# Two 32-byte pads that move the normalized inputs and the feed-forward tiles by 32 and 64 bytes

## The chip, the cores and the metric

One NeuronCore of a Trainium2 chip runs the kernel. The metric is the time of one execution on the device in microseconds (us): 2235.31 us is the median of three runs before the change (2234.43 to 2235.77).

## The reference

A sequence of 256 positions and a context of 256 positions, each of width 1024 in float32, go through two transformer layers and then a second block of two hybrid layers. A layer of the first block is feed-forward, attention, feed-forward, and every feed-forward (four in all) is

```
def _ffn_sublayer(h, mod, g_pre, g_post, w_in, w_out):
    shift, scale, gate = mod
    u = _modulate(_rmsnorm(h, g_pre), shift, scale)
    a, b = jnp.split(u @ w_in, 2, axis=-1)
    y = (jax.nn.silu(a) * b) @ w_out
    return h + MACARON_W * gate * _rmsnorm(y, g_post)
```

with an inner width of 2816. The first layer's attention is a differential one, the second's a neighbourhood one; shift, scale and gate come from a conditioning vector through large matrices (the "ada" work). The last feed-forward is computed for the sequence alone, the other three for sequence and context. The hybrid layers project a normalized input to several small mixers (latent attention, a gated delta rule, block attention), join their outputs and add the result. The output is the normalized sequence, 256 by 1024.

## The kernel before, in words

**The products.** Every large product is made in the float32r type from numbers that are split in two: a high part (a rounded copy, made by ScalarE) and a low part (what is left, made by VectorE; both in `split`, lines 155 and 156). `mm3` (line 190) then issues three matmuls: high by high and high by low on the same stationary tile, and then low by high on the low tile. All of them are recorded in `mm` (line 161), so the profile puts them at L164, L168 or L179, whatever their stage; the tiles' names tell them apart. The stationary operand of 128 by 128 is loaded anew for each matmul, so PE's matmuls (PE) and its weight loads (PEld) have the same count. The moving operand is 512, 258 or 256 columns wide, one float32r word a column, and lies in one unbroken run of a partition.

**Who is stationary and who moves.** In the feed-forward's first product (`part`, line 466), in the attention projections and in the hybrid layers' projections the weight tile `w` is stationary and the normalized input `u` moves. In the feed-forward's second product (`into`, line 500) `w` is stationary and the feed-forward's tile `b` moves. In the attention's output projection (`out_proj`, line 635) `w` is stationary and `o` moves. In `v_tiles` (line 602) it is the other way round: `u` is stationary and `w` moves.

**Stages.** A feed-forward for both halves first makes some inner tiles for the sequence alone (256 columns), then, when the context's input is normalized, for the context alone (256), then both at once (`wide`, 512); after 12 of 22 inner tiles it makes the first part of the second product (512), after the rest the remaining parts for each half (256). The last feed-forward and the hybrid layers move 256 columns, the last feed-forward's first product 258 (two more columns carry the shift). Weights come by SP's DMA queue into four raw tiles of 512 KB each and are split into eight `w` tiles.

**Where tiles lie.** SBUF space is given to pools in the order in which they are opened (lines 89 to 95), and each pool's tiles follow one another; a tile of any size takes a multiple of 32 bytes. So the small constants of the pool `cst` end at a multiple of 32, and all that follows starts there. By the program as it is built, a tile's start in its partition, modulo 128 bytes, is before the change:

| tiles | start modulo 128 |
|---|---|
| `w` (split weights) and `raw` | 64 |
| `u` (normalized inputs, pool `up`), `y` and `v` (pool `yp`), `c4`, `s`, `r256`, `r512` (pool `tmp`) | 64 |
| `b` of the feed-forward (opened by `space`, line 110) | 96 |
| `o`, `kl`, `qk`, `pT` of both attentions (opened by `space` too) | 96 |
| `ra`, `cb` (ada work, pool `cbp`) | 96 |
| `gd`, `sel`, `lvl` of the hybrid layers | 64 |
| `ident` | 32 |

All these tiles but the smallest have sizes that are multiples of 128 bytes, and the columns at which matmuls enter them too, so a matmul's moving operand starts at the tile's own remainder. PSUM's tiles are in a memory of their own.

**The order of work.** The order of instructions on each engine is that of the program; a tile's reuse waits for its last reader. The tiles named here are made once for each use, by `tile` of their pool.

Of the kernel before, what the change touches and what calls it, by code (L numbers as in the profile page):

```python
# [23 lines left out]
F = mybir.dt.float32  # L24
# [19 lines left out]
class Split:  # L44


    def __init__(self, hi, lo):
        self.hi, self.lo = hi, lo
# [35 lines left out]
class Net:  # L84
    def __init__(self, es, tc, I, O, stages=None, dump=None):
        self.tc, self.nc, self.I, self.O = tc, tc.nc, I, O
        self.stages, self.dump = stages, dump
        self.anchor = self.last_load = None
        self.cst = self.pool(es, "cst", 1)
        self.wp = self.pool(es, "wp", N_W)  # L90
        self.rawp = self.pool(es, "rawp", N_RAW)
        self.up = self.pool(es, "up", 8)
        self.yp = self.pool(es, "yp", 4)
        self.tmp = self.pool(es, "tmp", 3)
        self.col = self.pool(es, "col", 4)
        self.nps = self.pool(es, "nps", 1, space=bass.MemoryType.PSUM)
# [12 lines left out]
    @contextmanager  # L109
    def space(self, name, n):  # L110

        with ExitStack() as es:
            self.bp = self.pool(es, name, n)
            yield

# [1439 lines left out]
```

## Time and profile before

| | |
|---|---|
| median of the runs | 2235.31 us |
| the profiled execution, its own time | 2234.45 us |
| its span, first to last instruction | 2232.3 us |
| mean granted clock of TensorE, as a share of full speed | 0.993 |
| PE busy | 2169.9 us, 97% |
| VectorE (DVE) busy | 1589.2 us, 71% |
| ScalarE (ACT) busy | 1118.0 us, 50% |

A row of a group of instructions gives line, engine and operation, the tiles it writes and reads, shapes and count, then the busy time, the mean of one in ns, and the idle time ahead of them. A piece of the chain that ended last gives start, length (both us), engine, tile and line, and after "x" the number of instructions in it. Where the chain stays on PE, the length divided by the number is the pace, the time from one matmul's start to the next; the "mean ns of one" is longer, since a matmul is counted until its last result is out, while the next is already running.

### The profile page before, as it was taken

The page shows a single profiled execution, that of the slowest core. Times are in us where ns is not written, and L with a number is a line of the kernel's source. Part 1 is how long each engine was busy: PE and PEld are TensorE (multiplying, and loading weights), DVE is VectorE, ACT ScalarE, POOL GpSimd, SP SyncE. Part 2 cuts the span into 40 slices and gives each one's busy share as a digit, 9 for nine tenths or more (in the row PEclk, how much of TensorE's full clock was granted, in tenths as well). Part 3 has the DMA queues.
Part 4 walks back from the last instruction along what each step waited for, and adds up shares of the span by engine and source line. Part 5 has one row for each costly group of instructions (what it writes and reads, how often), then busy time and mean ns, then how long its engine had stood idle before and what let it go on. Part 6 is the DMA issues. An engine that isn't in the chain of part 4 may idle for free.

```text
span 2232.3 us, 33427 instructions
## 1 busy us (share of the span) xinstructions
PE 2169.9 (97%) x13010; PEld 1876.6 (84%) x13010; DVE 1589.2 (71%) x2899; ACT 1118.0 (50%) x1841; POOL 6.5 (0%) x33
## 2 busy tenths in 40 slices
PE   7999999999999999999999999999999989999998
PEld 3888889877789888889988889977789989888986
DVE  7877674869978876767844454956665668977985
ACT  4422223668867322236622223668754448457644
POOL 0000000000000000000000000000000000000000
PEclk9999999999999999999999999999999999999999
DMA  8555553431134655544554453432335543324321
GB/s 300 198 181 192 182 183 130 156 104 48 38 104 164 228 202 189 193 165 149 185 177 153 168 170 133 152 132 88 109 129 190 175 164 123 114 81 138 120 99 57
DMA packets 96166, 332.77 MB, mean 149 GB/s; under 512 B 12772, under 2 KB 15462, under 8 KB 96008
## 3 DMA queue, kind: packets, MB, share of 16 engines
q1 hardware_dynamic: 96008, 330.64, 43.5%
q8 instruction: 102, 1.67, 0.3%
q14 instruction: 56, 0.46, 0.1%
HBM read 329.55 MB, written 1.05 MB: 148 GB/s over the span
## 4 chain that ended last, share of the span: by engine, by line
PE 79%; ACT 9%; DVE 9%; issue 1%; DMA 1%; SPq 0%; DVEq 0%; ACTq 0%
PE ab L164 36%; PE ac L164 16%; PE ac L168 7%; PE pj L164 5%; PE ab L179 5%; PE gd L164 3%; PE n L164 2%; PE ab L168 2%; ACT w L155 2%; DVE w L156 1%; PE at L164 1%; DVE y L375 1%; ACT c L772 1%; PE gd L168 1%; PE pj L168 1%
## 5 line engine op out<-in xcount | busy, mean ns | idle before, releaser
L155 ACT ACTIVATE w<-raw 128x1024 fp32r<-128x1024 f32 x466 | 489.7, 1053 | 789.5 <-PE ab L164 269.8
L164 PE MATMUL ab<-u,w 128*128 128x512 f32 (+2 forms) x4320 | 870.9, 361 | 4.1 <-ACT u L438 4.1
L164 PEld LDWEIGHTS ab<-u,w 128*128 128x128 f32 x4320 | 728.8, 189 | 126.0 <-ACT u L438 4.5
L156 DVE TENSOR_TENSOR w<-raw,w 128x1024 fp32r<-128x1024 f32 x466 | 567.6, 1220 | 319.6 <-ACT w L155 312.7
L164 PE MATMUL ac<-b,w 128*128 128x512 f32 (+1 forms) x1152 | 235.9, 366 | 0.0
L164 PEld LDWEIGHTS ac<-b,w 128*128 128x128 f32 x1152 | 195.6, 188 | 39.6
L168 PE MATMUL ac<-b,w 128*128 128x256 f32 x1680 | 200.3, 280 | 0.0
L168 PEld LDWEIGHTS ac<-b,w 128*128 128x128 f32 x1680 | 198.2, 188 | 0.8
L164 PE MATMUL pj<-u,w 128*128 128x256 f32 (+1 forms) x1200 | 158.8, 288 | 5.6 <-ACT u L438 4.4
L293 DVE SCALAR_TENSOR_TENSOR ra<-ra,cb 128x1024 f32<-128x1024 f32 x130 | 158.3, 1222 | 5.1 <-ACT cb L1349 2.2
L164 PEld LDWEIGHTS pj<-u,w 128*128 128x128 f32 (+1 forms) x1200 | 148.2, 190 | 10.5 <-ACT u L438 5.0
L179 PE MATMUL ab<-u,w 128*128 128x256 f32 x1152 | 147.1, 289 | 9.1 <-ACT u L155 7.8
L179 PEld LDWEIGHTS ab<-u,w 128*128 128x128 f32 x1152 | 143.6, 196 | 10.7 <-ACT u L155 8.1
L293 DVE SCALAR_TENSOR_TENSOR c<-ra,cb 128x1024 f32<-128x1024 f32 x98 | 118.8, 1220 | 12.9 <-ACT cb L1349 6.4
L484 DVE TENSOR_TENSOR s<-s,ab 128x512 f32<-128x512 f32 (+1 forms) x78 | 47.1, 604 | 90.6 <-PE ab L164 90.0
L164 PE MATMUL ac<-w,u 128*128 128x512 f32 x384 | 90.4, 394 | 0.0
L164 PEld LDWEIGHTS ac<-w,u 128*128 128x128 f32 x384 | 71.7, 188 | 15.4 <-DVE u L156 0.4
L164 PE MATMUL n<-r,ones 128*128 128x256 f32 (+1 forms) x216 | 73.2, 449 | 7.4 <-DVE r L62 3.3
L155 ACT ACTIVATE b<-s 128x512 fp32r<-128x512 f32 (+1 forms) x100 | 53.5, 535 | 28.3 <-DVE s L484 21.2
L156 DVE TENSOR_TENSOR b<-s,b 128x512 fp32r<-128x512 f32 (+1 forms) x100 | 56.3, 563 | 3.1 <-ACT b L155 2.9
L164 PEld LDWEIGHTS n<-r,ones 128*128 128x128 f32 x216 | 36.5, 196 | 20.1 <-DVE r L62 9.6
L64 ACT ACTIVATE r<-h 128x512 f32<-128x512 f32 x56 | 35.0, 627 | 31.3 <-DVE h L379 10.6
(290 smaller groups left out, 2297.1 us busy)
## 6 DMA issues: line engine op xcount, KB each, us to landing
raw<-in_fin SPq DMA_DIRECT2D x194, 512.0 KB, 3.3
raw<-in_fout SPq DMA_DIRECT2D x112, 512.0 KB, 3.3
ra<-in_ada SPq DMA_DIRECT2D x72, 512.0 KB, 4.2
ra<-in_ada0r SPq DMA_DIRECT2D x58, 512.0 KB, 3.2
raw<-in_w SPq DMA_DIRECT2D x54, 512.0 KB, 3.3
raw<-in_da_qk SPq DMA_DIRECT2D x16, 512.0 KB, 3.2
raw<-in_na_qk SPq DMA_DIRECT2D x16, 512.0 KB, 3.3
raw<-in_w2o SPq DMA_DIRECT2D x16, 512.0 KB, 3.2
```

The costliest lines, as they stand in the source:

```text
L64: net.nc.scalar.activation(s, x, AF.Square)
L155: self.nc.scalar.activation(hi, x, AF.Copy)
L156: self.anchor = self.nc.vector.tensor_tensor(lo, x, hi.bitcast(F), op=OP.subtract).ins.name
L164: return mm(out, lhsT, rhs, start=start, stop=stop)
L168: ins = mm(out, lhsT, rhs, start=start and "first" not in bank, stop=stop and bank["done"] == n)
L179: ins = mm(out, lhsT, rhs, start=start, stop=stop)
L293: ins = nc.vector.scalar_tensor_tensor(junk, w, 1.0, self.cb[:, j], op0=OP.mult, op1=OP.mult, accum_out=self.mod[l][:, m, t, j:j + 1])
L375: ins = nc.vector.scalar_tensor_tensor(yy[:, t], yy[:, t], cols[:, k:k + 1], r, op0=OP.mult, op1=OP.mult)
L484: nc.vector.tensor_tensor(s, s, pb, op=OP.mult)
L772: nc.scalar.activation(e[:, j, :nk], s, AF.Exp, bias=mx[:, j:j + 1], accum_out=sm[:, j:j + 1])
```

## The change

Two pads of 8 float32 (32 bytes in each partition) are made as pools of their own, each with one small memset on GpSimd (POOL). The first stands in front of the pool `up`; everything that is opened later moves up by 32 bytes with it. The second stands in front of the feed-forward's pool and is made anew in each of the four feed-forwards; only `b` moves by it, a further 32 bytes. `w`, `raw` and the constants keep their places.

```
+        pad = self.pool(es, "pad", 1).tile([128, 8], F, name="pad", tag="pad")
+        tc.nc.gpsimd.memset(pad, 0.0)
         self.up = self.pool(es, "up", 8)
...
         with ExitStack() as es:
+            if name == "ffn":
+                pad = self.pool(es, "ffnp", 1).tile([128, 8], F, name="pad", tag="pad")
+                self.nc.gpsimd.memset(pad, 0.0)
             self.bp = self.pool(es, name, n)
```

So `u`, `y`, `v`, `c4`, `s`, `r256`, `r512` and the hybrid layers' `gd`, `sel`, `lvl` go from 64 to 96 modulo 128, `ra`, `cb` and the attentions' `o`, `kl`, `qk`, `pT` from 96 to 0, and `b` from 96 to 32.

## Rows read from the trace of the kernel before

**Rows 1.** The page: busy time of each engine, and the granted clock in 40 slices.
```profile
PE 2169.9 (97%) x13010; PEld 1876.6 (84%) x13010; DVE 1589.2 (71%) x2899; ACT 1118.0 (50%) x1841; POOL 6.5 (0%) x33
...
PEclk9999999999999999999999999999999999999999
```

**Rows 2.** Busy us (and count) of PE, PEld, DVE, ACT, POOL by stretch; granted clock.
```profile
60.00:400.00 340.00, 340.00 (x1706) 289.07 (x1706) 239.67 (x349) 108.05 (x145) 0.00 (x0) 1.00 0.52 178
...
1830.00:2060.00 230.00, 217.98 (x1578) 194.70 (x1579) 189.51 (x443) 146.29 (x247) 1.62 (x16) 0.99 0.33 111
```

**Rows 3.** The page: the chain that ended last, share of the span by line.
```profile
PE ab L164 36%; PE ac L164 16%; PE ac L168 7%; PE pj L164 5%; PE ab L179 5%; PE gd L164 3%; PE n L164 2%; PE ab L168 2%; ACT w L155 2%; DVE w L156 1%; PE at L164 1%; DVE y L375 1%; ACT c L772 1%; PE gd L168 1%; PE pj L168 1%
```

**Rows 4.** The chain in order of time, its longest pieces: start, length, instructions.
```profile
71.21 108.83 PE ab L164 x480
180.03 67.20 PE ac L164 x288
...
356.07 29.87 PE ac L168 x256
...
419.69 16.13 PE ac L164 x71
...
1072.02 40.31 PE ab L179 x336
...
1739.91 59.51 PE ab L164 x480
```

**Rows 5.** The chain in two short stretches: output projection, and gates of a hybrid layer.
```profile
641.73 4.55 PE ac L168 x39
...
1864.87 2.70 PE at L164 x23
```

**Rows 6.** Groups by line and form: matmuls with `u`, `b`, `w` or `o` moving.
```profile
L164 PE MATMUL ab<-u,w 128*128 128x512 f32 x3096 | 716.8, 390 | 0.0
L164 PE MATMUL ac<-b,w 128*128 128x512 f32 x864 | 202.1, 395 | 0.0
L168 PE MATMUL ac<-b,w 128*128 128x256 f32 x1680 | 200.3, 280 | 0.0
L164 PE MATMUL pj<-u,w 128*128 128x256 f32 x1152 | 152.2, 288 | 5.6 <-ACT u L438 4.4 <-DVE w L156 0.7 <-DVE r L1159 0.5
L179 PE MATMUL ab<-u,w 128*128 128x256 f32 x1152 | 147.1, 289 | 9.1 <-ACT u L155 7.8 <-DVE u L156 1.0 <-DVE w L156 0.2
L164 PE MATMUL ab<-u,w 128*128 128x258 f32 x1056 | 132.9, 286 | 4.1 <-ACT u L438 4.1
L164 PE MATMUL ac<-w,u 128*128 128x512 f32 x384 | 90.4, 394 | 0.0
L168 PE MATMUL ac<-o,w 128*128 128x256 f32 x384 | 47.6, 282 | 0.0
L164 PE MATMUL ac<-b,w 128*128 128x256 f32 x288 | 33.8, 279 | 0.0
L168 PE MATMUL gd<-u,w 128*128 128x256 f32 x192 | 29.9, 292 | 4.7 <-DVE w L156 2.7 <-ACT w L155 2.1
...
L168 PE MATMUL ab<-o,w 128*128 128x256 f32 x192 | 28.7, 298 | 2.3 <-ACT w L155 2.3
...
L164 PE MATMUL ab<-u,w 128*128 128x256 f32 x168 | 22.3, 282 | 0.0
```

**Rows 7.** Groups by line and form: VectorE with `c` or `ra`, and POOL's memsets.
```profile
L293 DVE SCALAR_TENSOR_TENSOR ra<-ra,cb 128x1024 f32<-128x1024 f32 x130 | 158.3, 1222 | 5.1 <-ACT cb L1349 2.2 <-DMA ra<-in_ada 0.5
L293 DVE SCALAR_TENSOR_TENSOR c<-ra,cb 128x1024 f32<-128x1024 f32 x98 | 118.8, 1220 | 12.9 <-ACT cb L1349 6.4 <-DMA ra<-in_ada0r 3.3 <-DMA ra<-in_ada 3.2
...
L1015 POOL MEMSET xp<- 128x3 f32 x24 | 2.4, 102 | 487.3 <-DVE r L1020 234.3 <-PE ac L168 223.0 <-DVE w L996 8.1
```

**Rows 8.** PE's transposes of line 200: nanoseconds least, median and most.
```profile
L200 PE MATMUL ac<-ident,e x128: 270/272/273, 1488.5 to 1602.7; 128*128 128x128 f32 x128
...
L200 PE MATMUL at<-ident,r x48: 270/272/333, 1969.8 to 2213.2; 128*128 128x128 f32 x48
```

## The prediction, made before the changed kernel was run

> **What bounds the kernel now.** I read the page's busy times first. PE is busy 97% of the span, VectorE 71%, ScalarE 50%, and the clock is granted in full in every slice, which is the 2.4 GHz level [rows 1]. By stretch it is the same: in the first feed-forward PE is busy in all of the 340 us while VectorE has 100 us to spare; in a hybrid layer PE still has 218 of 230 us, but with gaps [rows 2]. The shares of the chain say which work has to change for the end to move: it runs through PE's products of every kind, half of it through those with `u` and `b` moving [rows 3]. So only the pace of matmuls can matter much, and the reader should look at it, not at the mean of one.
>
> **The pace depends on where the moving operand starts.** The chain's long pieces stay on PE, so length by count is the pace [rows 4, 5]:
> - `u` moving from 64, 512 columns: 108.83 / 480 = 226.7 ns;
> - `b` from 96, 512 columns: 67.20 / 288 = 233.3 ns;
> - `u` from 64, 256 columns: 40.31 / 336 = 120.0 ns;
> - `b` from 96, 256 columns: 29.87 / 256 = 116.7 ns; `o` from 96: 4.55 / 39 = 116.7 ns;
> - `w` moving from 64 with `u` stationary, 512 columns: 16.13 / 71 = 227.2 ns.
>
> At 2.4 GHz 512 columns are 213.3 ns and 256 are 106.7 ns. From 64, then, a matmul costs some 13.4 ns over its columns at either width; from 96 it costs 20 ns at 512 and 10 ns at 256, that is, a share. That `o` goes with `b` and the moving `w` goes with `u`, though loop order and PSUM tiles differ, is what makes me put it down to the start. So 96 is worse than 64 for the wide matmuls by 6.6 ns, and better for the narrow ones by 3.3 ns.
>
> **The sum.** After the change `u` starts at 96, as `b` does now, with the same `w` under it; this half has its price in the rows.
> 1. *512 columns, `u` from 64 to 96.* 3,096 matmuls [rows 6]. Of these 2,592 are in three feed-forwards (the chain has six pieces like the first one, with 480, 480, 336, 480, 336 and 480), wholly on the path: 2,592 x 6.6 ns = +17.1 us. The other 504 are attention projections, between waits for ScalarE and VectorE; +3.3 us, and I take half: +1.7.
> 2. *256 columns, `u` from 64 to 96.* 1,152 with L179, 1,152 with `pj`, two groups of 192 (`gd` and a `pj` one) and two of 168 [rows 6]: 3,024 x 3.3 ns = -10.0 us. L179 holds 5% of the span's chain, some 112 us of 147 busy, and `pj` at L164 the same of 152 [rows 3, 6], so three quarters are on the path: -7.5. Ends: -4 (the feed-forwards alone) and -10.
> 3. *258 columns, `u` from 64 to 96.* 1,056 matmuls [rows 6]; the pace is 59.51 / 480 = 124.0 ns, with a gap at each change of tile in it [rows 4]. At most they come down to 116.7 x 258 / 256 = 117.6 ns, -6.8 us; nothing is the other end. I take the narrow ones' 3.3 ns: -3.5.
> 4. *`b` from 96 to 32.* 864 matmuls of 512 columns and 1,680 + 288 = 1,968 of 256 [rows 6], nearly all on the path. No float32r operand of before starts at 32. Below: no stream is faster than a column a cycle, so -(20 x 864 + 10 x 1,968) ns = -37 us. Above: another step as from 64 to 96 for the wide and the other way for the narrow, +6.6 x 864 + 3.3 x 1,968 = +12.2 us. Which row is nearest? Starts that are multiples of 64 (`u`, `w`) share one behaviour, and 32 and 96 are both 32 over such a multiple; a start that splits each piece of 64 bytes would do so alike at both. I take the row of 96: 0.
> 5. *`o` from 96 to 0.* 384 + 192 matmuls of 256 columns [rows 6]; by the same parity 0 goes with 64: 576 x 3.3 ns = +1.9 us; the other end is 0.
> 6. *`w` moving, `u` stationary from 64 to 96.* 384 matmuls [rows 6]. The moving start stays, so 0; if the stationary start counts as much, 384 x 6.6 ns = 2.5 us either way. Against that: the transposes move `ident` from 32, and take 272 ns with stationary `e` at 96 as with `r` at 64 [rows 8]. The remaining two-pass float32 matmuls take twice the time a column; I leave them at 0.
> 7. *VectorE, ScalarE, DMA.* The ada product costs 1,222 ns with its output at 96 and 1,220 with it at 64 [rows 7]; both engines have room [rows 2]; 0.
> 8. *The pads.* Five memsets, each by the row of the smallest ones 0.1 us [rows 7], on POOL, which is busy 6.5 us in all [rows 1]. Behind one in the queue stand the memsets of `kl` and `xp`; a feed-forward's pad may wait until what lay there before is free, and so may they, but attention or hybrid layers come after a whole feed-forward's work. If that cover were gone, it would be 5 x 0.1 us. 0.
>
> Sum: 17.1 + 1.7 - 7.5 - 3.5 + 0 + 1.9 = **+9.7 us**. The profiled execution's own 2234.45 us (its span and 2.2 us around it) becomes 2244.2; it lies 0.9 us under the median of the runs, so against that I say 2235.3 + 9.7 = **2245.0 us**, 0.43% slower. Two runs of this kernel that differ by under 0.2%, 4.5 us, cannot be told from no change.
>
> **Rivals.**
> - *32 is the best start of all (faster).* Place: the second product, `ac<-b,w`. The loss per column may grow with the start within 128 bytes, so that 32 is as far below 64 as 64 is below 96: 512 columns at 226.7 - 6.6 = 220.1 ns, -13.2 x 864 = -11.4 us; the narrow ones, where the loss is then less than at 96, at perhaps 113.4, -3.3 x 1,968 = -6.5. With the rest as above: 2245.0 - 17.9 = 2227.1 us. It decides from 9.7 us / 2,832 = 3.4 ns a matmul on. For it: 64 and 96 do differ by a share of the columns. Against it: the narrow ones are better at 96 than at 64, which no growth with the start explains; and with only 8 columns to load, `u` from 64 runs at 2.70 / 23 = 117.4 ns [rows 5], so part of the narrow 120 ns is the load, not the start. Chance 0.25.
> - *The start is not the cause (no change).* Then `b` is slower at 512 columns for its loop (a new PSUM tile after every six matmuls) and nothing moves: 2235.3 us. For it: all rows of `b` are of that loop. Against it: `w` moving changes its PSUM tile after every three, and has 227 ns. The Trainium skill says as much as this rival: its page "SBUF — State Buffer", section "Who interferes with whom", has PE with two independent read ports, one for the moving operand and one for the loads, and waiting on nobody, and its specifications know only lines of 16 bytes, of which 32, 64 and 96 are all multiples; "TensorE: Matmul & The Clock Gate", section "Wait — 56ns, not 53.3ns?", gives one pace for 512 columns, 215.7 ns. The trace agrees with neither, as it has 226.7 and 233.3 ns [rows 4]. Chance 0.15.
> - *32 is worse than 96 (slower still).* The price is the upper end of step 4: 2245.0 + 12.2 = 2257.2 us. For it: nothing but that two neighbouring starts already differ. Chance 0.13.
>
> **How the numbers follow.** My forecast has 0.47. Its own range is 2238 to 2250 us, from the ends of steps 1 to 3, 5 and 6. To leave out no more than 2 in 10 the range must reach the faster rival and most of the third: 2226 to 2256 us. Faster by over 0.2% comes from the first rival and a little of the forecast's edge (0.27); within 0.2% from the second and the forecast's lower end, should the narrow gains all count (0.18); slower from the rest (0.55).
>
> **What would show it.** In the profile after: `ab<-u,w` of 512 columns in pieces of 480 at 112.0 us where it was 108.8 shows step 1; the L179 piece of 336 at 39.2 us step 2; `ac<-b,w` still at 67.2 us for 288 and 29.9 us for 256 step 4. The forecast is wrong if the `u` pieces keep 226.7 ns (then the start alone is not the cause), or if `b` at 32 falls under some 230 ns at 512 or 113 ns at 256.

## The result, and the profile after

The changed kernel takes 2256.69 us (median of 4, 2254.71 to 2257.44) where the kernel before takes 2235.54 (4 runs, 2234.43 to 2237.47). The medians are 21.2 us apart; the ratio of the runs is lower, 1.0085 with an interval of 1.0073 to 1.0097, which is 19.0 us and 16.3 to 21.7. The forecast was 9.7 us slower; the range ended at 2256, and the rival "32 is worse than 96" had 2257.2.

The page after: PE has 24.4 us more to do than before [rows 1], the other engines the same, and the clock is at nine tenths or more in every slice, as before; its mean is 0.990 of full speed, where it was 0.993.

```profile
PE 2194.3 (97%) x13010; PEld 1880.1 (83%) x13010; DVE 1589.0 (70%) x2899; ACT 1118.4 (50%) x1841; POOL 6.9 (0%) x38
...
PEclk9999999999999999999999999999999999999999
```

The chain in order of time answers to [rows 4]. The program is five lines longer, so L164, L168 and L179 of before are L169, L173 and L184 here.

```profile
70.47 111.99 PE ab L169 x480
182.47 67.21 PE ac L169 x288
...
361.68 30.71 PE ac L173 x256
...
426.13 16.55 PE ac L169 x71
...
749.90 78.39 PE ab L169 x336
...
1086.58 39.20 PE ab L184 x336
...
1762.60 59.32 PE ab L169 x480
```

Line by line against before: wide `u` from 108.83 to 111.99 us; wide `b` as it was; narrow `b` from 29.87 to 30.71; the moving `w` of `v_tiles` from 16.13 to 16.55; narrow `u` from 40.31 to 39.20; the 258 columns from 59.51 to 59.32. The starts of the same pieces say where the time came: 0.7 us early at the first, then 2.4 us late, 5.6, 6.4, 14.6 at 1086.58 and 22.7 at 1762.60; the two spans are 23.4 us apart. So nearly all of it is lost in the first block; from the piece of 258 columns to the end, which is mostly the hybrid layers, the two traces differ by 0.7 us only, to which step 2 below comes back.

Groups by form, for wide `u`, the hybrid layers' projections and the attentions' output projections (columns as in [rows 6]), and the pads on POOL:

```profile
L169 PE MATMUL ab<-u,w 128*128 128x512 f32 x3096 | 735.6, 396 | 0.0
...
L169 PE MATMUL pj<-u,w 128*128 128x256 f32 x1152 | 149.3, 285 | 5.9 <-ACT u L443 4.4 <-DVE w L161 0.9 <-DVE r L1164 0.6
...
L173 PE MATMUL ac<-o,w 128*128 128x256 f32 x384 | 47.9, 282 | 0.0
...
L173 PE MATMUL ab<-o,w 128*128 128x256 f32 x192 | 30.6, 311 | 2.3 <-ACT w L160 2.3
...
L173 PE MATMUL gd<-u,w 128*128 128x256 f32 x192 | 30.5, 296 | 4.0 <-ACT w L160 2.1 <-DVE w L161 2.0
...
L117 POOL MEMSET pad<- 128x8 f32 x4 | 0.4, 109 | 393.5 <-DVE qk L761 209.2 <-PE ac L169 184.2
```

The pads cost 0.1 us each on an idle engine; that they wait is harmless, since the trace has no instruction that waits for them.

### The profile page after: what moved, and what is told of

The parts are those of the page before. It is cut to its first block, busy times and chain, and to the rows that moved or that the text cites. A ratio compares the mean times of both kernels' runs of the same rounds, so it can differ in the third digit from the quotient of the medians.

```text
span 2255.7 us, 33434 instructions
## 1 busy us (share of the span) xinstructions
PE 2194.3 (97%) x13010; PEld 1880.1 (83%) x13010; DVE 1589.0 (70%) x2899; ACT 1118.4 (50%) x1841; POOL 6.9 (0%) x38
## 4 chain that ended last, share of the span: by engine, by line
PE 80%; ACT 10%; DVE 7%; DMA 1%; issue 1%; SPq 0%; DVEq 0%; ACTq 0%
PE ab L169 36%; PE ac L169 15%; PE ac L173 10%; PE ab L184 5%; PE pj L169 4%; PE gd L169 3%; PE n L169 2%; ACT w L160 2%; PE at L169 1%; PE ab L173 1%; PE gd L173 1%; DVE w L161 1%; PE pj L173 1%; ACT w L707 1%; ACT c L777 1%
## 5 line engine op out<-in xcount | busy, mean ns | idle before, releaser
L169 PE MATMUL ab<-u,w 128*128 128x512 f32 (+2 forms) x4320 | 889.4, 364 | 4.1 <-ACT u L443 4.1
L169 PEld LDWEIGHTS ab<-u,w 128*128 128x128 f32 x4320 | 727.4, 188 | 145.6 <-ACT u L443 4.5
L169 PE MATMUL ac<-b,w 128*128 128x512 f32 (+1 forms) x1152 | 236.8, 367 | 0.0
L169 PEld LDWEIGHTS ac<-b,w 128*128 128x128 f32 x1152 | 196.8, 188 | 39.4
L173 PE MATMUL ac<-b,w 128*128 128x256 f32 x1680 | 205.7, 283 | 0.0
L173 PEld LDWEIGHTS ac<-b,w 128*128 128x128 f32 x1680 | 203.4, 188 | 0.8
L169 PE MATMUL pj<-u,w 128*128 128x256 f32 (+1 forms) x1200 | 155.9, 285 | 5.9 <-ACT u L443 4.4
L169 PEld LDWEIGHTS pj<-u,w 128*128 128x128 f32 (+1 forms) x1200 | 145.2, 187 | 11.1 <-ACT u L443 5.0
L184 PE MATMUL ab<-u,w 128*128 128x256 f32 x1152 | 144.2, 286 | 8.5 <-ACT u L160 7.2
L184 PEld LDWEIGHTS ab<-u,w 128*128 128x128 f32 x1152 | 140.7, 193 | 10.2 <-ACT u L160 7.5
L169 PE MATMUL ac<-w,u 128*128 128x512 f32 x384 | 92.5, 399 | 0.3
L169 PEld LDWEIGHTS ac<-w,u 128*128 128x128 f32 x384 | 71.7, 188 | 17.7 <-ACT u L160 0.7
L169 PE MATMUL n<-r,ones 128*128 128x256 f32 (+1 forms) x216 | 76.3, 465 | 7.2 <-DVE r L62 2.8
L169 PEld LDWEIGHTS n<-r,ones 128*128 128x128 f32 x216 | 38.4, 204 | 18.3 <-DVE r L62 6.1
```

The costliest lines, as they stand in the source:

```text
L169: return mm(out, lhsT, rhs, start=start, stop=stop)
L173: ins = mm(out, lhsT, rhs, start=start and "first" not in bank, stop=stop and bank["done"] == n)
L184: ins = mm(out, lhsT, rhs, start=start, stop=stop)
```

## The experiments

The theory to start with: not the moving operand's start sets the pace, but its distance from the stationary operand's, since in `v_tiles` only the stationary tile has moved and the pace still went from 227.2 to 16.55 / 71 = 233.1 ns. The rival is the forecast's own reason, the moving start alone. Where times are compared, each kernel ran on one chip with runs of the kernel before, which had medians of 2238.0 to 2238.6 us there; so the ratios count. Paces are read from the chain's pieces, length by count.

### The first pad alone

```
+        pad = self.pool(es, "pad", 1).tile([128, 8], F, name="pad", tag="pad")
+        tc.nc.gpsimd.memset(pad, 0.0)
         self.up = self.pool(es, "up", 8)
```

> Only the pad in front of the normalized inputs: u at 96, w still at 64, so u lies 32 over w; b and o at 0, that is 64 under w. Theory (the pace goes by the moving start less the stationary start, modulo 128): u of 512 columns 233.3 ns and v_tiles 233 ns as in the changed kernel; b of 512 columns some 233 ns, since it is not 0 over its weights; b of 256 columns as o at 0 in the changed kernel, 117.5 ns. Against the kernel before: +17.1 +1.7 +2.3 us for the wide ones, at most -7.5 for the narrow u, +1.6 for the narrow b: 2250 us, about 5 us under the changed kernel. Rival (the moving start alone, by its remainder modulo 64): b at 0 is as u at 64 was, 226.7 ns and 120.0 ns, 2253 us.

Measured: 1.0039 times before (1.0024 to 1.0053), +8.7 us, less than either theory had. The chain's pieces:

```profile
70.41 111.99 PE ab L166 x480
182.40 65.92 PE ac L166 x288
...
360.31 29.01 PE ac L170 x256
...
423.14 16.56 PE ac L166 x71
```

Wide `u` and the moving `w` are as slow as in the changed kernel (233.3 and 233.2 ns), so that loss belongs to the first pad alone. Wide `b`, now 64 over its weights, has 228.9 ns, a pace not seen before, between those of 64 and 96; narrow `b` has 113.3 ns, faster than any narrow piece before. Parity modulo 64 would have given 226.7 and 120.0. From the start of each kind of work to the start of the next, the feed-forwards are 9.5 us longer than before in this trace: wide `u` 17.0 more, wide `b` 3.8 less, narrow `b` 2.2 less, narrow `u` and the 258 columns 1.5 less. So it is the faster `b` that the theory lacked.

### Only `b` moved, to 32

In this and the kernels like it, only the number of float32 in the second pad differs, and the first pad is left out.

```
+            if name == "ffn":
+                pad = self.pool(es, "ffnp", 1).tile([128, 16], F, name="pad", tag="pad")
+                self.nc.gpsimd.memset(pad, 0.0)
             self.bp = self.pool(es, name, n)
```

> Only b moves, from 96 to 32 (64 bytes in front of the feed-forward's pool), u and all else as before. Theory: the whole loss of b in the changed kernel is here, 1,968 x 3.3 ns = +6.5 us, and nothing else: 2242 us; u keeps 226.7 ns at 512, b has 233.3 ns at 512 and 120.0 ns at 256. Rival (part of the loss comes from other tiles that moved with the first pad, or from the memsets on GpSimd): under 2239 or over 2245 us.

Measured: 1.0012 (1.0002 to 1.0021), +2.7 us, under the 6.5 that the paces give. The paces themselves are the expected ones:

```profile
70.63 108.83 PE ab L167 x480
179.46 67.21 PE ac L167 x288
...
355.51 30.72 PE ac L171 x256
...
387.53 13.90 PE ac L171 x116
...
419.95 16.12 PE ac L167 x71
```

`u` keeps 226.7 ns, `b` has 233.4 and 120.0. So the narrow loss of `b` comes with its place 96 over the weights. That it is under 6.5 us has its reason in the chain. Of the 480 narrow matmuls of a feed-forward 256 are in the long piece. Among the others PE was not the engine that set the time in the kernel before: there the chain goes over to VectorE, which splits weights and makes the next input.

```profile
389.09 1.22 DVE w L156
...
395.14 1.14 DVE w L156
...
402.20 12.37 PE ac L168 x106
```

With the slower `b` it stays on PE (the piece of 116), so part of the loss fills time in which PE had waited. From the start of the long narrow piece to the start of `v_tiles` it was 419.69 - 356.07 = 63.62 us before [rows 4] and is 419.95 - 355.51 = 64.44 here, 0.8 more, where 480 x 3.3 ns would be 1.6. The other two feed-forwards of this kind have 0.8 too and the last 1.3, so 3.7 in all; the interval says 0.4 to 4.7.

### Everything moved, the weights too

```
+        pad = self.pool(es, "pad", 1).tile([128, 8], F, name="pad", tag="pad")
+        tc.nc.gpsimd.memset(pad, 0.0)
         self.wp = self.pool(es, "wp", N_W)
```

> One pad of 32 bytes in front of the pool of w: w and u both at 96, b and o at 0. All differences between moving and stationary starts are those of the kernel before (u 0, b and o +32), while u's own start is that of the changed kernel. Theory (the difference counts): the time of the kernel before, 2235.5 us, with 226.7 ns for u of 512 columns and 120.0 ns at 256, 233.3 and 116.7 ns for b. Rival (the moving operand's own start counts): u of 512 columns at 233.3 ns, +19 us, and b at 0 in some new place; 2245 us or more.

Measured: 1.0001 (0.9991 to 1.0010).

```profile
69.78 108.83 PE ab L166 x480
178.61 67.20 PE ac L166 x288
...
354.65 29.87 PE ac L170 x256
...
418.26 16.14 PE ac L166 x71
...
1071.36 40.31 PE ab L181 x336
```

Every piece has the length of before to 0.01 us, with `u` at 96 as in the changed kernel and `b` at 0. This settles it for the paces: a shift of both operands by 32 bytes costs nothing, a change of the distance between them does. The rival falls, and with it the reason of the forecast.

One doubt is left by these edits: `raw` lies at the same remainder as `w` in all kernels, so the distance could be one to what DMA, ScalarE and VectorE read and write there. The changed kernel's first wide piece of `u` speaks against it. Two stretches of 9 us in it hold the same 40 matmuls (first count after PE's busy time), with VectorE busy 7.93 or 5.28 us and the DMA engines 0.88 or 0.41 of the time (the last figure but one):

```profile
82.00:91.00 9.00, 9.00 (x40) 7.25 (x39) 7.93 (x14) 2.77 (x4) 0.00 (x0) 1.00 0.88 289
...
145.00:154.00 9.00, 9.00 (x40) 7.25 (x39) 5.28 (x8) 1.61 (x2) 0.00 (x0) 1.00 0.41 137
```

### `b` level with its weights, modulo 128

The pad of the second kernel with 24 float32, where that had 16.

> Only b moves, from 96 to 64 (96 bytes in front of the feed-forward's pool), where its weights w start too. Theory: b then goes as u does before: 226.7 ns at 512 columns, 864 x -6.6 ns = -5.7 us, and 120.0 ns at 256, 1,968 x 3.3 ns = +6.5 us; in sum 2236.3 us, no change that can be told. Rival (the loop of the second product makes the 233.3 ns): b of 512 columns keeps 233.3 ns and the time is 2235.5 or, with the narrow ones slower, 2242 us.

Measured: 1.0006 (0.9997 to 1.0016). The time is what the theory gave, but not for its reason (that the slower narrow pieces cost less in time than their paces give was so in the second kernel too):

```profile
178.14 67.19 PE ac L167 x288
...
354.15 30.71 PE ac L171 x256
```

Wide `b` keeps 233.3 ns, as the rival had it. Yet the loop is not the cause either, since the first kernel had 228.9 ns in the same loop. What was wrong is the period: `b` at 64 modulo 128 lay 128 bytes over `w`, and 128 is not as 0, which the next kernels bear out.

### All distances in steps of 32

Four kernels, the second pad with 8, 32, 48 and 56 float32; the last three have one time each, so only their paces are read.

> Only b moves, by 32 bytes: it starts 64 bytes over its weights, as in the first of these experiments, while u stays level with w. Theory (the distance of the two starts sets the pace): b at 228.9 ns for 512 columns and 115.8 ns for 256, as measured there, and nothing else changes: 864 x -4.4 ns and 1,968 x -0.9 ns = -5.6 us, 0.25% faster than the kernel before. Rival (b's pace there came from the other tiles' places): 233.3 and 116.7 ns, no change.

> Only b moves, by 128 bytes, so that it starts at 96 modulo 128 again but 160 bytes over its weights where it was 32 over them. Theory A (only the distance modulo 128 counts): exactly the kernel before, 233.3 ns at 512 columns and 116.7 ns at 256, within 0.2% of its time. Theory B (the distance counts over at least 256 bytes, since b at 64 and w at 64, 128 bytes apart, had 233.3 ns where u and w, 0 apart, have 226.7): another pace at one width at least.

> Only b moves, by 192 bytes: 224 over its weights, which modulo 256 is 32 under them. In the changed kernel the moving w lay 32 under the stationary u and had 233.2 ns at 512 columns. Theory B with a period of 256: the same here, 233.3 ns, and some 118 ns at 256 columns. Modulo 128 alone (theory A) it would be like 96 over, 233.3 and 120.0 ns, as b in the changed kernel.

> Only b moves, by 224 bytes: exactly 256 over its weights. Theory B with a period of 256: as u over w before, 226.7 ns at 512 columns and 120.0 ns at 256; 864 x -6.6 + 1,968 x 3.3 ns = +0.8 us. With a longer period: anything else, 233.3 ns most likely, as at all other distances but 0 and 64.

And with 40 float32, run later:

> Only b moves, by 160 bytes: 192 over its weights, the one distance of the eight modulo 256 not yet seen. If the two streams meet in the same way on either side, it is like 64 over: 228.9 ns at 512 columns and 113 to 118 ns at 256. If only 0 and 64 are good: 233.3 ns at 512 columns and 117 to 120 ns at 256.

The pieces of each, in this order (64, 160, 224, 256, then 192 over `w`):

```profile
179.77 65.94 PE ac L167 x288
...
354.56 30.15 PE ac L171 x256
```

```profile
180.72 67.47 PE ac L167 x288
...
357.00 30.38 PE ac L171 x256
```

```profile
180.17 67.20 PE ac L167 x288
...
356.20 30.29 PE ac L171 x256
```

```profile
180.18 65.28 PE ac L167 x288
...
354.25 30.71 PE ac L171 x256
```

```profile
178.02 67.20 PE ac L167 x288
...
354.04 30.15 PE ac L171 x256
```

Together with the kernels above, the paces of a matmul of `b` in the first feed-forward (for the first line of `u` in the kernel before, its narrow pace from the third feed-forward):

| moving start over the stationary start, bytes | 512 columns, ns | 256 columns, ns |
|---|---|---|
| 0 (`u`) | 226.7 | 120.0 |
| 32 | 233.3 | 116.7 |
| 64 | 228.9 and 229.0 | 113.3 in one kernel, 117.8 in another |
| 96 | 233.4 | 120.0 |
| 128 | 233.3 | 120.0 |
| 160 | 234.3 | 118.7 |
| 192 | 233.3 | 117.8 |
| 224 | 233.3 | 118.3 |
| 256 | 226.7 | 120.0 |

A distance of 256 is exactly as 0, and 128 and 160 are not as 0 and 32: the distance counts over 256 bytes. For wide matmuls 0 is best, 64 next, all others alike to half a percent. The narrow ones have no such order, and the two values at 64 say that they have no single pace for a distance.

With all of `b` 64 over its weights and nothing else changed (8 float32 in the pad) the kernel takes 0.9977 of the time before (0.9968 to 0.9986), 5.1 us less. The expected 5.6 us came out, but in part by luck. Its narrow part was wrong: the 115.8 ns "as measured there" is in no piece of the first kernel, which had 113.3, and here it is 117.8. By the starts in the chain wide `b` gives -3.8 us and narrow `b` +1.1, in sum -2.7, which is less than the least that the interval allows (3.1); where the rest comes from stays open.

### Wide and narrow `b` apart

The feed-forward's pool is opened twice, with a pad of 56 float32 for the first 12 inner tiles, which are only read 512 wide, and none for the other 10.

```
-        with self.space("ffn", 12):
+        with ExitStack() as sp:
+            sp.enter_context(self.space("ffn", 12, 56 if halves == 2 else 0))
...
+            if halves == 2:
+                sp.close()
+                sp.enter_context(self.space("ffn2", 10))
             for f in range(FA, FT):
                 wide(f)
```

> In the three feed-forwards for both halves the first 12 inner tiles of b (read 512 columns wide) lie 256 bytes over their weights, and the last 10 (read 256 wide) 32 bytes over them, as all did before; nothing else moves. Theory: 226.7 ns for the wide ones, 864 x -6.6 ns = -5.7 us, while the narrow ones keep 116.7 ns: 2230 us where the kernel before has 2235.5, 0.25% faster, and a little under the kernel with all of b 64 over. Rival (the second pool's tiles, which lie across two of the first's, wait for later readers and PE stops there): a stop of some us at each of the three hand-overs, no gain.

Measured: 0.9971 (0.9961 to 0.9981), 6.5 us less.

```profile
180.54 65.28 PE ac L167 x288
...
354.62 29.87 PE ac L171 x256
...
1704.04 34.56 PE ac L167 x288
```

The wide pieces have 226.7 ns, and PE goes from one piece into the next without a stop (180.54 + 65.28 = 245.82, where the wide `u` then starts, and the same at the two other hand-overs), so the rival's waits are not there. The last line is the last feed-forward, narrow and with `b` 32 over `w` at the very addresses of before: 120.0 ns, where before it had 116.7, in this piece of its chain:

```profile
1706.31 33.61 PE ac L164 x288
```

### The same, with narrow `b` 64 over

As above with pads of 8 float32 in the second pool and in the last feed-forward.

> As the kernel with wide b 256 over its weights, but the narrow b lies 64 over them and not 32, in the last feed-forward too. Theory (the distance alone gives the narrow pace): one pace for all the narrow pieces, and the same as with all of b 64 over. Rival (a narrow stream settles into one of several steady paces by how it is entered, since the same distance of 64 and the same addresses gave pieces of 29.01 us and of 30.15 us for 256 matmuls): pieces at 113.3 in one feed-forward and at 117 to 120 ns in another. Time: the wide ones give -5.7 us, the narrow ones between -6.7 us (113.3 ns) and +2.2 us (117.8 ns) against the kernel before: 2223 to 2232 us where that has 2235.5.

Measured: 0.9969 (0.9957 to 0.9981), 6.9 us less, the lowest ratio of all, though its interval and those of the two kernels above overlap. By the starts in the chain this kernel should gain 4.6 us and the one before it 4.5; both measured more, with intervals (4.2 to 9.6 and 4.3 to 8.7 us) that just hold these sums.

```profile
180.70 65.28 PE ac L167 x288
...
354.78 30.15 PE ac L171 x256
...
1705.69 33.92 PE ac L167 x288
```

All shown narrow pieces have 117.8 ns here; of the two, the theory's single pace is what this kernel shows, while the pieces of 29.01 and 34.56 us above speak for the rival. The narrow pace was not brought under control: 113.3 ns was seen in the first kernel alone.

## Why the prediction was wrong, step by step

Its direction was right and its size was not: 19.0 us by the ratio and 21.2 by the medians, against 9.7. The terms follow; what a term cost is read, where it can be, from the start of a kind of work to the start of the next in the two chains.

1. *512 columns of `u`*: right. The six pieces grew by 3.16 us (four of 480) and 2.20 us (two of 336, 78.39 where it was 76.19), 17.0 us together; +17.1 was forecast. The whole group's busy time rose from 716.8 to 735.6 us, so the attentions' 504 matmuls have 1.8 of it, where 1.7 was taken.
2. *256 columns of `u`*: the pace was right (39.20 / 336 = 116.7 ns), how much of it reaches the end was not: -7.5 was forecast. The feed-forwards' chains show 1.1 us of it, in that one piece. In the hybrid layers, where the forecast had -3.8 for 1,152 + 2 x 192 matmuls, it seems to be missing: cut at the same work in both, before and then after:

```profile
1830.00:2232.30 402.30, 378.65 (x2744) 337.31 (x2744) 326.44 (x786) 239.84 (x411) 2.23 (x22) 0.99 0.31 104
```

```profile
1852.70:2255.70 403.00, 378.75 (x2744) 335.95 (x2744) 326.50 (x786) 240.14 (x411) 2.23 (x22) 0.98 0.31 104
```

   But these two did not have the same clock: 0.99 and 0.98 of full speed, the figure behind POOL's. The same work at 0.98, first with everything moved (so `u` level with `w`), then with the first pad alone (`u` 32 over):

```profile
1832.00:2236.50 404.50, 382.40 (x2744) 339.93 (x2744) 326.38 (x786) 239.80 (x411) 2.21 (x22) 0.98 0.31 104
```

```profile
1840.40:2243.40 403.00, 378.65 (x2744) 335.37 (x2744) 325.99 (x786) 239.75 (x411) 2.21 (x22) 0.98 0.31 104
```

   The other traces agree. From the end of the piece of 258 columns to the end of the span, the eleven kernels with `u` level take 432.9 to 434.5 us where the clock of that stretch is 0.99 (five traces) and 435.1 to 436.5 where it is 0.98 (six); the two with `u` 32 over take 433.6 and 433.8, both at 0.98. So at a like clock the faster `u` is worth 1.3 to 2.9 us there, and in the profiled pair the lower clock hid it. These are single traces, and the clock has two digits, so the size is rough.
3. *258 columns of `u`*: -3.5 was forecast; 59.51 to 59.32 us in 480 matmuls is nearly nothing, and the other 576 show no more (0.4 us in all by the starts). The step took over the narrow ones' 3.3 ns without a row for it.
4. *`b` from 96 to 32*: the step that failed first. "I take the row of 96: 0" was right for 512 columns and wrong for 256, where the pace rose by 3.3 ns, half of the upper end: 1,968 x 3.3 ns = 6.5 us if all of it were on the path. "Nearly all on the path" was wrong too: by the starts it cost 3.7 us, as in the kernel that moves `b` alone (measured 0.4 to 4.7). Its ground, that 32 and 96 share a parity modulo 64, is refuted: with the weights moved along, every piece had its old length.
5. *`o`*: +1.9 forecast. `ac<-o,w` grew by 0.3 us in busy time, [rows 6] against the groups after. `ab<-o,w` grew by 1.9, but that is no sign of the place: with the first pad alone `o` lies as in the changed kernel, and the group has 28.7 us as before.
6. *`w` moving, `u` stationary*: 0 forecast, and the pace behind the end of 2.5 us was true: 16.13 to 16.55 us for 71, 5.9 ns each, 384 x 5.9 = 2.3 us at most; the two pieces of 71 on the chain show 0.8 of it. The transposes of [rows 8], which I set against it, were no evidence: they are another kind of matmul.
7. and 8. *Other engines, pads*: right, 0.

The forecast fell short by 9.3 us of the ratio (6.6 to 12.0 by its interval) and by 11.5 of the medians. By these readings 3.7 of it is step 4, 3.1 step 3, 3.5 to 5.1 step 2 (7.5 less 1.1 and less 1.3 to 2.9) and 0.8 to 2.3 step 6; up to 1.6 goes off, which step 5 had too much. That is 9.5 to 14.2 us, enough for either, and not closer than that: the two attentions, where PE has gaps, vary by 1.8 and 4.3 us among traces in which nothing of theirs was moved.

Of the rivals, "32 is the best start" fell with both widths of `b`: the wide kept its pace, the narrow became slower. "32 is worse than 96" came nearest in its time and had only a part of the reason: the pace of the wide `b` did not change. "The start is not the cause" is false as it was put, but half right: the moving start alone is not. The page "SBUF — State Buffer" of the Trainium skill gives PE two independent read ports, for the moving operand and for the weight loads (section "Who interferes with whom"). The runs here do not agree with what would follow, that the place of one does not matter to the other: in `v_tiles` the moving operand's place was unchanged, and it went from 227.2 to 233.1 ns when only the stationary tile lay elsewhere.

The general fault: all rows of before had the weights at one place, so that a moving start and a distance could not be told apart in them; the forecast chose one, and named the other only as the doubt of step 6.

## What to carry to other kernels

In a stream of float32r matmuls that load new weights each time, ask where the moving tile lies against the stationary one, modulo 256 bytes: a distance of 0 was 6.6 ns better per matmul of 512 columns than most others, 3% of such a stream, and a pad of 32 bytes in front of one pool decided it. Move the two together and nothing happens, so a pad that shifts a whole stack of pools helps or hurts only where it parts two operands. For narrow matmuls the piece must be measured in its place, and a change of pace counts only where PE holds the chain: of the narrow `b`'s 6.5 us 3.7 were there. Where PE has gaps, compare stretches at the same granted clock before you say that a gain is missing.

## What the runs showed that had not been expected

- The pace depends on the distance of the two operands over 256 bytes: 226.7 ns at 0 and 256, 228.9 at 64, 233.3 at 128, for the same 512 columns.
- A narrow stream runs at one of several steady paces, and the addresses alone do not say which. With `b` 64 over `w` at the same addresses, 256 matmuls took 29.01 us behind a slower wide stream and 30.15 us behind a faster one; with `b` 32 over, 288 matmuls of the last feed-forward took 33.61 and 34.56 us in two kernels. Within a piece the pace is steady (45, 45, 45, 45, 45 matmuls in five stretches of 5 us before, 47, 47, 47, 47, 46 with the first pad alone). What chooses it stays open: the stream ahead is one guess, but in the last feed-forward that was of the same kind and at the same addresses in both kernels. Why the two reads disturb each other stays open too.
